# An attention loop with its score matmuls in the halves of the array's rows, four key tiles to a batch

## The chip, the cores and the metric

The kernel runs on one core of one Trainium2 chip. Its time is device time in microseconds (us). A core has five engines that run side by side and wait for one another through semaphores: TensorE (PE in the profile, with its weight loads as PEld), VectorE (DVE), ScalarE (ACT), GpSimd (POOL) and SyncE (SP), which here only issues transfers. Matmul results land in PSUM, eight banks of 128 partitions by 512 floats.

## What is computed

Two layers of a bidirectional encoder on 2048 tokens of width 1024. The part that the change touches is the attention: eight query heads of width 64, two key/value heads, all 2048 keys for every query.

```python
def _attention(q, k, v):
    ...
        scores = jnp.einsum('bqkgd,bskd->bkgqs', qb, k,
                            preferred_element_type=jnp.float32) * scale
        p = jax.nn.softmax(scores, axis=-1).astype(v.dtype)
        return jnp.einsum('bkgqs,bskd->bqkgd', p, v)
```

In each layer a combined input projection comes first, then the attention with a Fourier mixer beside it, then the output projection with a layer norm. All numbers are float32.

## The kernel before

**Stages.** `in_proj` projects the tokens (L302 to L304 and L329 to L331), writes the rotated queries to the DRAM tiles `q1`, keeps keys (`kk1`, `kk2`) and values (`V`) on the chip, and near its end runs `first_unit`, which computes the first row maxima of the attention between its own matmuls. `attention` follows, with `fourier` as a background generator: one step of it per batch, until it is through. `out_proj` comes last. Inside `attention` the queues of PE, ACT, DVE and POOL run in program order (a manual schedule); elsewhere a scheduler sets the order.

**Units and batches.** A unit is two query heads that share a key/value head, for 512 queries (`CH`): 16 units in a layer. Each unit has 16 key tiles of 128 keys, taken in six batches of 3, 3, 2, 3, 3 and 2 (`BATCHES`). For each batch PE does, one block behind the other: the scores of the batch's tiles, as many row-maxima pairs of a later unit, and the weighing by V of the tiles of the batch before.

**Scores.** Queries and keys are split into a rounded high part and a low remainder (`hi`, `lo`). A score tile of one head is two matmuls over all 128 rows of the array (L854, L855). The first has the high key twice, in rows 0 to 63 and 64 to 127, against a query tile `qq1` that holds high and low parts in its two halves. The second has the low key in one half and a row of ones in the other, against `qq2`, which holds the high query and, in one row, the negated row maximum (the guard row). ACT takes the exponential out of PSUM (L856).

**Maxima.** `row_max` computes an approximate score block with 64 rows of the array for one head and the other 64 for the other head (L789, one pair of matmuls), into two PSUM banks; DVE takes their maxima (L793). They run 6 pairs (`LEAD`) ahead of the unit whose scores come next. When a unit's 16 pairs are through, `guard_row` transposes the result on PE (L804), DVE copies it (L806), and two small transfers write it into `qq2` (L808).

**Weighing.** `weigh` multiplies the exponentials by V into 64 columns per head (L866, one PSUM bank `psC`), and adds the exponentials up for the denominators: four of a unit's tiles on DVE, twelve on POOL (L874 for the first sum, L876). In a layer's last unit all 16 are DVE's. `sums` (L885) and `finish` (L899 to L913) turn the sums into the divided result during the next unit.

**PSUM.** Seven banks (`A`) are handed out in turn to scores, maxima, sums, guard and Fourier blocks. An allocation waits until the one seven before it has been read. The eighth (`C`) holds the weighed sum of a unit.

**Names that the change touches.** `q_load` and `q_copy` (L765 to L781) load query tiles, `fourier_mix_mats` loads `fm` (L583) for four small matmuls (L591) at the end of `in_proj`.

Of the kernel before, what the change touches and what calls it, by code (L numbers as in the profile page):

```python
# [13 lines left out]
P = 128  # L14
# [24 lines left out]
class Trunk:  # L39
# [34 lines left out]
    def setup(self):  # L74
# [10 lines left out]
        self.zero = self.const("zero", [P, 4])  # L85
        nc.gpsimd.memset(self.zero, 0.0)
# [316 lines left out]
    def do_q(self, l, grp, tabs):  # L403
        def fn(ps, s0):
            qn = self.t("XA", [P, 2, 256])
            self.norm_rope(qn, ps, 4, tabs, s0 % 8)
            self.later.append(lambda: q_trans(s0 // 4, slice(s0 % 4 * P, s0 % 4 * P + 2 * P), qn))

        def q_trans(ch, sl, qn):

            nc = self.nc
            pt = self.p("C", (P, 2, 2, P))
            for r in range(2):
                for s2 in range(2):
                    nc.tensor.transpose(out=pt[:, r, s2, :], in_=qn[:, s2, r * P:(r + 1) * P], identity=self.ident)
            hi = self.t("EV", [P, 2, 2 * P], F32R)
            lo = self.t("EV", [P, 2, 2 * P], F32R)
            self.split(hi, lo, pt.rearrange("p r s n -> p r (s n)"), act=True)
            for h in range(2):
                r, o = slice(h * HD, (h + 1) * HD), slice((1 - h) * HD, (2 - h) * HD)  # L420
                nc.sync.dma_start(self.q1[ch][grp][r, :, h, sl], hi.bitcast(F32)[r])
                nc.sync.dma_start(self.q1[ch][grp][o, :, h, sl], lo.bitcast(F32)[r])
        return fn

    def do_kv(self, l, tabs):
        def fn(ps, s0):
# [16 lines left out]
            nc.vector.tensor_tensor(kl[:, :, :, HD:], k4, khf[:, :, :, 0:HD], ALU.subtract)  # L443
            kl3 = kl.rearrange("p a b d -> p (a b) d")
            nc.vector.tensor_copy(kl3[:, :, 0:1], self.ones[:, 0:4].unsqueeze(2))
            nc.vector.tensor_copy(kl3[:, :, 1:HD], self.zero.unsqueeze(2).to_broadcast([P, 4, HD - 1]))
# [313 lines left out]
    LEAD = 6  # L760
    BATCHES = ((0, 1, 2), (3, 4, 5), (6, 7), (8, 9, 10), (11, 12, 13), (14, 15))
    NBT = len(BATCHES)

    def q_load(self, u):

        src = self.q1[u["ch"]][u["pr"] // 2][:, u["pr"] % 2]
        u["qq1"] = [self.t("TAB", [P, CH], F32R) for _ in range(2)]
        for h in range(2):
            self.nc.sync.dma_start(u["qq1"][h].bitcast(F32), src[:, h, :])
        u["qq2"], u["mx"] = [], [self.small("mx", [P, 4, 4]) for _ in range(2)]  # L770
        u["nm"] = self.small("nm", [P, 2, 4], F32R, bufs=3)

    def q_copy(self, u, h):

        src = self.q1[u["ch"]][u["pr"] // 2][:, u["pr"] % 2, h, :]
        q2 = self.t("QS", [P, CH], F32R)
        for r in ([slice(0, P)] if h else [slice(0, HD), slice(HD, P)]):
            dr = r if h else slice(HD - r.start, P - r.start)
            self.nc.sync.dma_start(q2.bitcast(F32)[dr], src[r])
        u["qq2"].append(q2)  # L780

    def row_max(self, u, i):
# [4 lines left out]
        for h in range(2):  # L787
            r = slice(h * HD, (h + 1) * HD)
            nc.tensor.matmul(pss[h], u["qq1"][h][r, s * P:(s + 1) * P], self.kk1[u["kv"]][kc][r], start=True, stop=True)  # L789

        def reduce():
            for h in range(2):
                nc.vector.tensor_reduce(out=u["mx"][h][:, s, kc:kc + 1], in_=pss[h], axis=AX.X, op=ALU.max)  # L793
            if i == 15:
                for h in range(2):
                    nc.vector.tensor_reduce(out=u["nm"][:, h, :], in_=u["mx"][h], axis=AX.X, op=ALU.max, negate=True)
                self.gq.append(u)
        return reduce

    def guard_row(self, u):  # L800
# [6 lines left out]
        for h in range(2):  # L807
            nc.sync.dma_start(u["qq2"][h].bitcast(F32)[0:1, :], nt.bitcast(F32)[4 * h:4 * h + 4, :])  # L808

    def max_before(self, i):  # L810

        for ui, u in enumerate(self.units):
# [3 lines left out]
            elif o in (8, 10):  # L816
                self.q_copy(u, o // 2 - 4)

    def max_pairs(self, pairs):

        while self.gq:
            self.guard_row(self.gq.pop(0))
        todo = [self.row_max(self.units[j // 16], j % 16) for j in pairs if 0 <= j < 16 * len(self.units)]
        for reduce in todo:
            reduce()

    def first_unit(self, l):
        self.units = [dict(ch=ch, pr=pr, kv=pr // 2) for ch in range(NCH) for pr in range(NPAIR)]
        for i in range(-6, NKT + self.LEAD, 2):
            self.max_before(i)  # L830
            self.max_before(i + 1)
            self.max_pairs((i, i + 1))
            yield

# [8 lines left out]
    DVE_KT = (0, 3, 8, 11), range(NKT)  # L843

    def scores(self, u, kt):
# [5 lines left out]
        ks = slice((kt % 4) * P, (kt % 4 + 1) * P)  # L851
        for h in range(2):
            ps = self.p("A")
            nc.tensor.matmul(ps, self.kk1[kv][kt // 4][:, ks], u["qq1"][h], start=True, stop=False)  # L854
            nc.tensor.matmul(ps, self.kk2[kv][kt // 4][:, ks], u["qq2"][h], start=False, stop=True)  # L855
            nc.scalar.activation(pt[:, h, :], ps, AF.Exp, scale=HD ** -0.5)  # L856

    def weigh(self, u, kt):
# [8 lines left out]
        w = "d" if kt in self.DVE_KT[u is self.units[-1]] else "p"  # L867
        eng = nc.vector if w == "d" else nc.gpsimd
# [25 lines left out]
    def finish(self, u, k):  # L894
# [5 lines left out]
        elif k == 3:  # L900
# [4 lines left out]
            for h in range(2):  # L905
                nc.sync.dma_start(u["sm"][h * HD:(h + 1) * HD, :], d[h * CH:(h + 1) * CH].partition_broadcast(HD))
        elif k == 4:
            nc.vector.tensor_tensor(u["y"], u["y"], u["sm"], ALU.mult)
        elif k == 5:
# [5 lines left out]
    def attention(self, l):  # L915
        self.yat = {}
        n = len(self.units)
        for g in range((n + 1) * self.NBT):
            ui, b = divmod(g, self.NBT)
            u = self.units[ui] if ui < n else None  # L920
            tiles = self.BATCHES[b]
            pairs = [NKT * (ui + 1) + self.LEAD + kt for kt in tiles]
            for j in pairs:
                self.max_before(j)
            if ui and b == 2:
                self.sums(self.units[ui - 1])
            if ui == n - 1 and b == 0:
# [3 lines left out]
            if u:  # L931
                for kt in tiles:
                    self.scores(u, kt)
            self.max_pairs(pairs)
            if 0 < g <= n * self.NBT:
                v, c = divmod(g - 1, self.NBT)
                for kt in self.BATCHES[c]:
                    self.weigh(self.units[v], kt)
            if u and b == 4:
                u["ga"] = self.t("EV", [P, CH])  # L940
                self.nc.sync.dma_start(u["ga"], self.ga[u["pr"]][u["ch"]])
            if ui:
                self.finish(self.units[ui - 1], b)
# [222 lines left out]
```

## Time and profile before

| what | value |
|---|---|
| median of 3 runs | 2721.76 us (2720.47 to 2722.68) |
| profiled execution, its own time | 2718.48 us |
| its span, first to last instruction | 2716.6 us |
| mean granted TensorE clock | 0.995 |
| busy PE / DVE / ACT / POOL | 2664.5 / 1821.2 / 891.0 / 1032.7 us |

How to read the rows that stand further down: a row of the chain of waits is the start in us, the length in us, and what the end of the program hung on at that time; "x12" counts records, and a float32 matmul of the weighing has two. A row of the windows gives, for a stretch, each engine's busy time and its count of instructions. A row of the groups gives the count, the busy time in us, the mean of one in ns, and behind a bar the idle time before it with what ended it. The shape "64\*128" behind a matmul is the part of the array that it uses, rows by columns; the program's tiles "psA" are the seven PSUM banks.

### The profile page before, as it was taken

The numbers are of one execution on the slowest core, as the hardware profiler recorded it, in microseconds if no ns is written. First come the engines' busy times: TensorE is split into PE (matmuls) and PEld (weight loads), VectorE is DVE, ScalarE is ACT, GpSimd is POOL, SyncE is SP. The second block draws the span as 40 slices with busy tenths as digits, with TensorE's granted clock in tenths as the row PEclk, the third lists the DMA queues.
The fourth block names the chain that finished last, engine by engine and source line by source line (L and its number), as shares of the span: only waits on it lengthen the run. The fifth ranks groups of instructions, "written<-read, shape, count | busy, mean of one in ns | idle before, by whom it ended". The sixth has DMA issues, their size and how long they took to land.

```text
span 2716.6 us, 36918 instructions
## 1 busy us (share of the span) xinstructions
PE 2664.5 (98%) x13748; PEld 1867.2 (69%) x13748; DVE 1821.2 (67%) x3072; ACT 891.0 (33%) x1789; POOL 1032.7 (38%) x597
## 2 busy tenths in 40 slices
PE   7999999999999999999999999999999999999998
PEld 5987898765555555557898889887565555554686
DVE  6655673457788788786785347534678888778655
ACT  3321421133444444430232124211444444444200
POOL 0200020035786777703331001100558777774134
PEclk9999999999999999999999999999999999999999
DMA  9754362333221111144446123522323111111332
GB/s 302 225 138 149 108 189 72 98 101 121 80 58 44 48 48 48 36 129 156 147 132 186 55 94 98 151 79 85 111 74 105 48 48 47 45 31 51 121 132 93
DMA packets 192516, 277.34 MB, mean 102 GB/s; under 512 B 40400, under 2 KB 103248, under 8 KB 191824
## 3 DMA queue, kind: packets, MB, share of 16 engines
q1 hardware_dynamic: 192336, 274.98, 33.1%
q8 instruction: 108, 1.77, 0.3%
q14 instruction: 72, 0.59, 0.1%
HBM read 213.68 MB, written 69.48 MB: 104 GB/s over the span
## 4 chain that ended last, share of the span: by engine, by line
PE 91%; DVE 4%; DMA 2%; issue 1%; POOL 1%; ACT 1%; SPq 0%; POOLq 0%; DVEq 0%; ACTq 0%
PE psC L866 16%; PE psA L854 9%; PE psA L329 8%; PE psA L330 8%; PE psA L331 8%; PE psA L855 8%; PE psA L789 6%; PE psA L1028 4%; PE psA L1026 4%; PE psA L1027 4%; PE psA L302 3%; PE psA L304 3%; PE psA L303 3%; PE psA L885 1%; PE psA L706 1%
## 5 line engine op out<-in xcount | busy, mean ns | idle before, releaser
L793 DVE TENSOR_REDUCE mx<-psA 128x1 f32<-128x512 f32 x1024 | 632.9, 684 | 238.5 <-PE psA L789 236.3
L876 POOL TENSOR_TENSOR WH<-WH,XA 128x1024 f32<-128x1024 f32 x150 | 362.5, 2417 | 211.1 <-ACT XA L856 208.4
L854 PE MATMUL psA<-TAB,KK 128*128 128x512 f32 x1024 | 421.8, 412 | 0.0
L855 PE MATMUL psA<-QS,KK 128*128 128x512 f32 x1024 | 403.3, 394 | 0.0
L329 PE MATMUL psA<-H,WH 128*128 128x512 f32 x1008 | 397.9, 395 | 0.0
L330 PE MATMUL psA<-H,WH 128*128 128x512 f32 x1008 | 393.4, 390 | 0.0
L331 PE MATMUL psA<-H,WL 128*128 128x512 f32 x1008 | 393.0, 390 | 0.0
L876 POOL TENSOR_TENSOR WH<-WH,WL 128x1024 f32<-128x1024 f32 x150 | 361.4, 2409 | 63.2 <-ACT WL L856 53.8
L856 ACT ACTIVATE XA<-psA 128x512 f32<-128x512 f32 x512 | 281.0, 611 | 307.0 <-PE psA L855 226.3
L856 ACT ACTIVATE WL<-psA 128x512 f32<-128x512 f32 x512 | 281.6, 615 | 161.2 <-PE psA L855 161.0
L854 PEld LDWEIGHTS psA<-TAB,KK 128*128 128x128 f32 x1024 | 192.3, 188 | 155.2 <-issue 87.2
L866 PE MATMUL psC<-XA,V 128*64 128x512 f32 x1024 | 271.3, 608 | 5.8 <-DVE EV L899 5.8
L866 PE MATMUL psC<-WL,V 128*64 128x512 f32 x1024 | 267.8, 601 | 0.0
L128 DVE TENSOR_TENSOR WL<-WR,WH 128x512 fp32r<-128x512 f32 (+2 forms) x272 | 126.0, 500 | 210.0 <-ACT WH L125 204.5
L874 POOL TENSOR_TENSOR WH<-WL,XA 128x1024 f32<-128x1024 f32 x30 | 71.0, 2366 | 446.1 <-DVE mx L793 378.4
L329 PEld LDWEIGHTS psA<-H,WH 128*128 128x128 f32 x1008 | 189.6, 188 | 46.3 <-issue 7.4
L302 PE MATMUL psA<-WH,H 128*128 128x256 f32 x768 | 219.8, 287 | 0.0
L125 ACT ACTIVATE WH<-WR 128x512 fp32r<-128x512 f32 (+2 forms) x280 | 119.4, 479 | 305.3 <-PE psA L330 112.1
L855 PEld LDWEIGHTS psA<-QS,KK 128*128 128x128 f32 x1024 | 192.2, 188 | 37.7
L304 PE MATMUL psA<-WH,H 128*128 128x256 f32 x768 | 216.4, 284 | 0.6 <-DVE H L128 0.6
L303 PE MATMUL psA<-WL,H 128*128 128x256 f32 x768 | 216.8, 283 | 0.0
L331 PEld LDWEIGHTS psA<-H,WL 128*128 128x128 f32 x1008 | 189.3, 188 | 39.8
(215 smaller groups left out, 4010.5 us busy)
## 6 DMA issues: line engine op xcount, KB each, us to landing
WR<-in_w_in SPq DMA_DIRECT2D x176, 256.0 KB
WR<-in_w_ada SPq DMA_DIRECT2D x64, 256.0 KB
q<-EV SPq DMA_DIRECT2D x128, 128.0 KB
TAB<-q SPq DMA_DIRECT2D x64, 256.0 KB
H<-dft SPq DMA_DIRECT2D x64, 256.0 KB
XA<-in_x SPq DMA_DIRECT2D x24, 512.0 KB
XA<-x SPq DMA_DIRECT2D x20, 512.0 KB
dft<-in_k_dft SPq DMA_DIRECT2D x32, 256.0 KB
```

Source lines behind the costliest of these rows:

```text
L302: nc.tensor.matmul(ps[:, s2, :], hh[b][:, sl], w1, start=(b == 0), stop=False)
L303: nc.tensor.matmul(ps[:, s2, :], hh[b][:, sl], w2, start=False, stop=False)
L304: nc.tensor.matmul(ps[:, s2, :], hl[b][:, sl], w1, start=False, stop=(b == NB - 1))
L329: nc.tensor.matmul(ps, w1, hh[b], start=(b == 0), stop=False)
L330: nc.tensor.matmul(ps, w1, hl[b], start=False, stop=False)
L331: nc.tensor.matmul(ps, w2, hh[b], start=False, stop=(b == NB - 1))
L793: nc.vector.tensor_reduce(out=u["mx"][h][:, s, kc:kc + 1], in_=pss[h], axis=AX.X, op=ALU.max)
L854: nc.tensor.matmul(ps, self.kk1[kv][kt // 4][:, ks], u["qq1"][h], start=True, stop=False)
L855: nc.tensor.matmul(ps, self.kk2[kv][kt // 4][:, ks], u["qq2"][h], start=False, stop=True)
L856: nc.scalar.activation(pt[:, h, :], ps, AF.Exp, scale=HD ** -0.5)
L866: nc.tensor.matmul(u["pv"][h * HD:(h + 1) * HD, :], v, pt[:, h, :], start=(kt == 0), stop=(kt == NKT - 1))
L876: eng.tensor_tensor(acc[w], acc[w], pt, ALU.add)
```

## The change

The scores of both heads of a tile are computed side by side. Four terms, high key by high query, high key by low query, low key by high query, and a selector row by the guard row, are each a pair of matmuls, one head in rows 0 to 63 and the other in rows 64 to 127. Two PSUM banks of a tile so fill at the same time. Query tiles are kept by part (high, low) and not by head, the guard row lies in a third tile `g`, and a constant `sel` picks it. Batches are four tiles, four batches to a unit, and inside a batch score tiles (S) and maxima pairs (M) go in the order S S M S M S M M; the maxima lead by 8 pairs. POOL's additions are issued with the scores and not with the weighing, DVE adds the last tile of each batch, and `finish` is spread over the four batches and the first of the unit behind. Outside the attention the queries are written in two transfers and not four, the low key is written to both halves, and the tile `fm` has one buffer and not two.

```diff
+        self.sel = self.const("sel", [P, P], F32R)
...
-            for h in range(2):
-                r, o = slice(h * HD, (h + 1) * HD), slice((1 - h) * HD, (2 - h) * HD)
-                nc.sync.dma_start(self.q1[ch][grp][r, :, h, sl], hi.bitcast(F32)[r])
-                nc.sync.dma_start(self.q1[ch][grp][o, :, h, sl], lo.bitcast(F32)[r])
+            for j, t in enumerate((hi, lo)):
+                nc.sync.dma_start(self.q1[ch][grp][:, :, j, sl], t.bitcast(F32))
...
-            fm = self.small("fm", [P, HD], bufs=2)
+            fm = self.small("fm", [P, HD], bufs=1)
...
-    LEAD = 6
-    BATCHES = ((0, 1, 2), (3, 4, 5), (6, 7), (8, 9, 10), (11, 12, 13), (14, 15))
-    NBT = len(BATCHES)
+    LEAD = 8
+    ORDER = "SSMSMSMM"
+    BATCH = len(ORDER) // 2
+    NBT = NKT // BATCH
...
+    def guard_load(self, u):
+
+        u["g"] = self.t("QS", [P, CH], F32R)
+        self.nc.sync.dma_start(u["g"].bitcast(F32), self.q1[u["ch"]][u["pr"] // 2][:, u["pr"] % 2, 0, :])
...
+    def guard_rows(self):
+
+        for e in list(self.gq):
+            e[1] -= 1
+            if not e[1]:
+                self.guard_row(e[0])
+                self.gq.remove(e)
...
-    DVE_KT = (0, 3, 8, 11), range(NKT)
+    DVE_KT = (3, 7, 11, 15), range(NKT)
...
+        k1, k2, (q1, q2) = self.kk1[kv][kt // 4][:, ks], self.kk2[kv][kt // 4][:, ks], u["q"]
+        pss = [self.p("A") for _ in range(2)]
+        terms = (k1, q1), (k1, q2), (k2, q1), (self.sel, u["g"])
+        for i, (k, q) in enumerate(terms):
+            for h in range(2):
+                r = slice(h * HD, (h + 1) * HD)
+                nc.tensor.matmul(pss[h], k[r], q[r], start=i == 0, stop=i == len(terms) - 1)
         for h in range(2):
-            ps = self.p("A")
-            nc.tensor.matmul(ps, self.kk1[kv][kt // 4][:, ks], u["qq1"][h], start=True, stop=False)
-            nc.tensor.matmul(ps, self.kk2[kv][kt // 4][:, ks], u["qq2"][h], start=False, stop=True)
-            nc.scalar.activation(pt[:, h, :], ps, AF.Exp, scale=HD ** -0.5)
+            nc.scalar.activation(pt[:, h, :], pss[h], AF.Exp, scale=HD ** -0.5)
+        self.add(u, kt, pt, "p")
...
+            at = {"S": 0, "M": 0}
+            for c in self.ORDER:
+                if c == "M":
+                    self.max_pairs((pair + at[c],))
+                elif u:
+                    self.scores(u, first + at[c])
+                at[c] += 1
```

On PE, in the middle of a layer's attention, the end of one batch before the change: L854 and L855 are a head's two score matmuls, L789 the maxima, L866 the weighing.

```order
L854 MATMUL psA_9354<-TAB_8713,KK_778 128x512
L855 MATMUL psA_9354<-QS_9047,KK_779 128x512
L789 MATMUL psA_9358<-KK_3260,TAB_9049 128x512
L789 MATMUL psA_9359<-KK_3260,TAB_9050 128x512
L789 MATMUL psA_9362<-KK_3491,TAB_9049 128x512
L789 MATMUL psA_9363<-KK_3491,TAB_9050 128x512
L789 MATMUL psA_9366<-KK_778,TAB_9049 128x512
L789 MATMUL psA_9367<-KK_778,TAB_9050 128x512
L866 MATMUL psC_9101<-XA_9285,V_3488 64x512 x2
L866 MATMUL psC_9101<-WL_9294,V_3488 64x512 x2
L854 MATMUL psA_9394<-TAB_8712,KK_778 128x512
L855 MATMUL psA_9394<-QS_8991,KK_779 128x512
```

The same place on PE in the changed kernel: L860 is a score matmul (two heads alternate, psA_10166 and psA_10167), L786 the maxima, L873 the weighing.

```order
L786 MATMUL psA_10160<-KK_1001,TAB_9906 128x512
L860 MATMUL psA_10166<-TAB_9110,KK_3244 128x512
L860 MATMUL psA_10167<-TAB_9110,KK_3244 128x512
L860 MATMUL psA_10166<-TAB_9111,KK_3244 128x512
L860 MATMUL psA_10167<-TAB_9111,KK_3244 128x512
L860 MATMUL psA_10166<-TAB_9110,KK_3245 128x512
L860 MATMUL psA_10167<-TAB_9110,KK_3245 128x512
L860 MATMUL psA_10166<-QS_9506,sel 128x512
L860 MATMUL psA_10167<-QS_9506,sel 128x512
L786 MATMUL psA_10178<-KK_3242,TAB_9906 128x512
L786 MATMUL psA_10179<-KK_3242,TAB_9906 128x512
L786 MATMUL psA_10184<-KK_3471,TAB_9906 128x512
```

Maxima now stand between score tiles, and a tile is eight matmuls of half the rows where it was four of all rows; the weighing (four tiles of it) follows once per batch.

On SP, where the weights of the last projection groups are loaded, the rows around `fm` (L583) in the changed kernel; before, both loads of this layer stood ahead of the middle of `in_proj`, one behind the other.

```order
L272 DMA WR_5463<-in_w_in 128x2x256
L272 DMA WR_5469<-in_w_in 128x2x256
L583 DMA fm_5055<-in_f_mix 128x64
L519 DMA yc_3_139<-EV_4901 128x512
L777 DMA QS_6504<-q_0_1_88 128x512
```

The layer's second `fm` load stands here, some 200 rows later than the first, since its only buffer is read until PE has run the first two L591 matmuls.

## Rows read from the trace of the kernel before

**Rows 1.** The page's first part: busy time, share, instructions.
```profile
PE 2664.5 (98%) x13748; PEld 1867.2 (69%) x13748; DVE 1821.2 (67%) x3072; ACT 891.0 (33%) x1789; POOL 1032.7 (38%) x597
```

**Rows 2.** Windows: six units without Fourier; and the last unit of layer 0.
```profile
843.24:1066.24 223.00, 223.00 (x1065) 114.60 (x1066) 178.77 (x253) 103.28 (x204) 158.02 (x67) 1.00 0.16 44
1165.00:1190.00 25.00, 25.00 (x114) 11.39 (x112) 24.33 (x32) 11.12 (x22) 0.00 (x0) 0.94 0.38 121
```

**Rows 3.** Chain of waits, 843 to 881 us, about one unit.
```profile
843.24 1.87 PE psC L866 x8
...
848.06 0.06 PE psA L804
848.12 1.34 PE psA L789 x4
...
854.27 0.67 PE psA L789 x4
854.93 2.73 PE psC L866 x12
857.66 0.43 PE psA L854
858.09 0.24 PE psA L855
...
860.46 0.23 PE psA L855
860.69 0.90 PE psA L789 x6
...
870.05 1.00 PE psA L885 x16
```

**Rows 4.** Chain of waits, 636 to 646 us: a Fourier step (L706 to L708) before scores.
```profile
637.08 0.43 PE psA L706
...
639.80 0.23 PE psA L708
640.03 0.23 PE psA L854
```

**Rows 5.** Groups of instructions in the six units of rows 2.
```profile
L793 DVE TENSOR_REDUCE mx<-psA 128x1 f32<-128x512 f32 x193 | 119.3, 684 | 37.2 <-PE psA L789 36.5
L856 ACT ACTIVATE XA<-psA 128x512 f32<-128x512 f32 x96 | 52.7, 611 | 63.8 <-PE psA L855 39.6 <-POOL WH L876 24.2
L876 DVE TENSOR_TENSOR WH<-WH,WL 128x1024 f32<-128x1024 f32 x6 | 19.4, 3225 | 0.0
L876 DVE TENSOR_TENSOR WH<-WH,XA 128x1024 f32<-128x1024 f32 x6 | 10.7, 1782 | 0.0
```

**Rows 6.** Timeline: DVE and POOL additions, around 857 and 1150 us.
```profile
856.87 2.39 POOL L876 TENSOR_TENSOR WH<-WH,WL 128x1024 f32<-128x1024 f32 x1
857.13 3.20 DVE L876 TENSOR_TENSOR WH<-WH,WL 128x1024 f32<-128x1024 f32 x1
...
1147.73 3.26 POOL L876 TENSOR_TENSOR WH<-WH,WL 128x1024 f32<-128x1024 f32 x1
1149.23 2.31 DVE L908 TENSOR_TENSOR EV<-EV,HS 128x512 f32<-128x512 f32 x1 [0.50 <-DMA HS<-rc]
```

**Rows 7.** The maxima's weight loads, 860.6 to 861.6 us: ns min/median/max.
```profile
L789 PEld LDWEIGHTS psA<-KK,TAB x6: 182/184/186, 860.6 to 861.0; 64*128 64x128 f32 x6
```

**Rows 8.** Timeline: a score matmul, the next weight load, and its exponentials.
```profile
845.37 0.39 PE L855 MATMUL psA<-QS,KK 128*128 128x512 f32 x1
845.38 0.19 PEld L854 LDWEIGHTS psA<-TAB,KK 128*128 128x128 f32 x1
...
845.86 1.08 ACT L856 ACTIVATE WL<-psA 128x512 f32<-128x512 f32 x2 [2.75 <-PE psA L855]
```

**Rows 9.** Timeline of SP, 843 to 850 us: small transfers of a unit.
```profile
846.83 0.32 SPq L903 DMA_DIRECT2D rc<-rc  x1
848.26 1.10 SPq L906 DMA_DIRECT2D HS<-rc  x2
849.46 0.63 SPq L808 DMA_DIRECT2D QS<-HS  x1
```

**Rows 10.** Windows: a wait of PE and a stretch behind it.
```profile
1160.60:1163.40 2.80, 0.00 (x0) 0.00 (x0) 1.28 (x3) 0.80 (x2) 0.00 (x0) 1.00 0.25 91
1165.00:1167.00 2.00, 2.00 (x8) 0.30 (x4) 1.90 (x3) 0.00 (x0) 0.00 (x0) 0.50 0.34 100
```

More of the change, by code (lines that the diff above doesn't have):

```diff
@@ L442, in fn @@
             nc.vector.tensor_copy(kh[:, :, :, HD:], k4)
[L443 to L446, printed above, removed]
+            for j in range(2):
+                nc.vector.tensor_tensor(kl[:, :, :, j * HD:(j + 1) * HD], k4, khf[:, :, :, 0:HD], ALU.subtract)
             self.later.append(lambda: k_trans(ch, slice(s * P, s * P + 2 * P), kh, kl))
@@ L788, in row_max @@
             r = slice(h * HD, (h + 1) * HD)
-            nc.tensor.matmul(pss[h], u["qq1"][h][r, s * P:(s + 1) * P], self.kk1[u["kv"]][kc][r], start=True, stop=True)
-        def reduce():
+            nc.tensor.matmul(pss[h], u["q"][0][r, s * P:(s + 1) * P], self.kk1[u["kv"]][kc][r], start=True, stop=True)
+        for h in range(2):
+            nc.vector.tensor_reduce(out=u["mx"][h][:, s, kc:kc + 1], in_=pss[h], axis=AX.X, op=ALU.max)
+        if i == 15:
             for h in range(2):
[L793 to L798, printed above, removed]
+                nc.vector.tensor_reduce(out=u["nm"][:, h, :], in_=u["mx"][h], axis=AX.X, op=ALU.max, negate=True)
+            self.gq.append([u, 2])
     def guard_row(self, u):
@@ L815, in max_before @@
                 self.q_load(u)
-            elif o in (8, 10):
-                self.q_copy(u, o // 2 - 4)
+            elif o == 8:
+                self.guard_load(u)
     def max_pairs(self, pairs):
[L821 to L825, printed above, removed]
+        for j in pairs:
+            if 0 <= j < 16 * len(self.units):
+                self.row_max(self.units[j // 16], j % 16)
     def first_unit(self, l):
@@ L917, in attention @@
         n = len(self.units)
-        for g in range((n + 1) * self.NBT):
+        for g in range((n + 2) * self.NBT):
             ui, b = divmod(g, self.NBT)
             u = self.units[ui] if ui < n else None
[L921 to L925, printed above, removed]
+            first = self.BATCH * b
+            pair = NKT * (ui + 1) + self.LEAD + first
+            for j in range(self.BATCH):
+                self.max_before(pair + j)
+            if 0 < ui <= n and b == 2:
                 self.sums(self.units[ui - 1])
+            self.guard_rows()
             if ui == n - 1 and b == 0:
@@ L930, in attention @@
             self.background()
[L931 to L934, printed above, removed]
+            at = {"S": 0, "M": 0}
[5 more added lines that the diff above has]
+                at[c] += 1
             if 0 < g <= n * self.NBT:
                 v, c = divmod(g - 1, self.NBT)
-                for kt in self.BATCHES[c]:
-                    self.weigh(self.units[v], kt)
-            if u and b == 4:
+                for j in range(self.BATCH):
+                    self.weigh(self.units[v], self.BATCH * c + j)
+            if u and b == 2:
                 u["ga"] = self.t("EV", [P, CH])
                 self.nc.sync.dma_start(u["ga"], self.ga[u["pr"]][u["ch"]])
-            if ui:
-                self.finish(self.units[ui - 1], b)
+            for back in (1, 2):
+                if 0 <= ui - back < n:
+                    self.finish(self.units[ui - back], b + self.NBT * (back - 1))
     def wout_consts(self, l):
```

38 lines of the change are left out of this document (19 added, 19 removed).

## Prediction

> **What bounds the kernel now.** I read the page's busy shares first: PE is busy 98% of the span, DVE 67% [rows 1]. Then the windows, because shares mix stages: the change works inside the attention, and six of its units without Fourier work take 223.00 us, 37.17 each, with PE busy for all of it, DVE for 178.77 / 6 = 29.8 and POOL for 26.3 us a unit [rows 2]. So PE sets the pace there, and the question is what of PE's 37.17 us is not work. The chain of waits tells it [rows 3]. A score matmul costs 0.23 to 0.24 us behind another, but 0.43 when it is the first behind the weighing. Two pairs of maxima take 0.67 us and three take 0.90: 0.23 a pair, two heads side by side, plus 0.20 for coming in. Four records per tile of the weighing give 1.87 us for two tiles and 2.73 for three: 0.86 a tile, plus 0.15. The 0.20 is no price of a first matmul as such: scores that follow a Fourier step, which uses the whole array as they do, cost 0.23 at once, while the Fourier step behind the weighing paid 0.43 [rows 4]. So **each change of the array's shape costs PE 0.15 to 0.20 us**, and a batch has three of them: 18 a unit. In the last unit of a layer, however, DVE has all the additions and is busy 24.33 of 25.00 us [rows 2]; there PE's saving buys nothing.
>
> Put together, the rows rebuild the unit. A batch of three: 0.43 + 11 x 0.235 + 0.90 + 2.73 = 6.65; of two: 0.43 + 7 x 0.235 + 0.67 + 1.87 = 4.62; four and two of them are 35.8; sums 1.00, guard 0.06, and 0.44 that one batch waits before its maxima (1.34 where others take 0.90): 37.3, against 37.17 measured.
>
> **The changed unit.** Scores and maxima now have one shape, 64 rows by 128, so a batch has two changes of shape and a unit has eight. I carry one batch along from its start. A pair of half-array matmuls is taken at 0.235 us, the maxima's price. A tile is four pairs, 0.94, as much as its four whole-array matmuls before, so **the work itself saves nothing**. With 0.20 for coming in, tiles one and two end at 1.14 and 2.08, the first maxima at 2.31, tile three at 3.25, the second maxima at 3.48. ACT sees a result about 0.26 after its matmul's slot (start 845.37, slot 0.23, ACT at 845.86 [rows 8]) and takes 52.7 / 96 = 0.55 for an exponential [rows 5]: 1.40 to 2.50 for tile one, to 3.60 for tile two. Tile four wants to begin at 3.48, but its first bank is the eleventh handed out, so it needs the fourth, tile two's second head, read at 3.60: it begins at about 3.65, **a new wait of 0.17 a batch**. It ends at 4.59, the last two maxima at 5.06, and the weighing at 5.06 + 0.15 + 4 x 0.86 = 8.65. DVE takes 119.3 / 193 = 0.62 for a maximum [rows 5]: from 2.57 to 7.55 for the eight, then its addition.
>
> That addition needs care. DVE's addition beside POOL's took 3.20: POOL's ended at 859.26 and DVE's 1.07 later [rows 6]; those in another place took 10.7 / 6 = 1.78 [rows 5]. So DVE's addition waits for the POOL one under way and then takes 1.07. POOL's three additions of a batch, 2.39 each, run from 2.5 to about 9.7, so DVE's ends at 10.8, 2.1 into the next batch and before that batch's first maxima at 2.57. With the short pieces of `finish` DVE is free by 3.0, and the bank that waits for the first maximum is wanted at 3.65. DVE so hides, with half a microsecond to spare; if that cover goes, PE waits at tile four.
>
> Unit: 4 x 8.65 + 1.00 for sums + 0.26 for the guard transpose, which now has a shape of its own between weighing and scores = 35.9. Against the 37.3 rebuilt from the same rows that is **1.4 us less a unit**. It holds for 14.5 of a layer's 16 units (in the second half of the fifteenth no maxima are left, and the last is DVE's), so 29 units: -40.6 us.
>
> **What the change adds.** Fourier matmuls use the whole array; they used to lead into scores of the same shape, now 16 steps a layer (eight small and eight large, of the generator) pay one more change: 32 x 0.20 = +6.4. The second `fm` load now waits for PE's first two L591 matmuls, and PE, next in order, waits for it. A small transfer of the profile takes 1.43 us from its issue to that of the one that needs its data (846.83 to 848.26 [rows 9]); the bounds are 1.4 and 2.8 with a busy queue. After a PE wait of 2.80 us the granted clock stood at 0.50, the lower level, 1.2 GHz, from 1165 to 1167 [rows 10], at least 1 us more. I take 2.5 a layer, +5.0, between +2.8 and +8. One more step of maxima in `in_proj` is +0.4 a layer, +0.8.
>
> Hidden: POOL's additions are issued a batch earlier, DVE loses small copies in `in_proj` and queries are written in half as many transfers; none of these stands in the chain. The guard row has less room. Its transpose begins a unit's last batch, DVE copies it at about 2.7, and SP has the reciprocals' transfers ahead of it: 846.83 to 849.46 is 2.63 [rows 9]. From 2.4 that makes 5.0, 1.3 to issue two, about 1.4 to land: 7.7, while the first selector matmul comes at 8.9 + 0.9. Two us are left; before it was about six.
>
> **Sum.** -40.6 + 6.4 + 5.0 + 0.8 = -28.4. The profiled execution's own time, 2718.48, becomes 2690.1; the median of the runs lies 3.28 above that execution, so I forecast **2693**. Bounds of this case: no wait at tile four (29 x 4 x 0.17 = 20), half-array pairs at 0.23 (29 x 64 x 0.005 = 9), and the small load at 1.4, together 2662; pairs at 0.243 (29 x 80 x 0.008 = 19) and the large load at 2.8 plus clock, 2715.
>
> **Rivals.** *Nothing gained.* Maxima show two or three pairs in a row, never twenty. If each of 80 pairs a unit costs 0.247, 29 x 80 x 0.012 = 28 us are gone: 2721. Against it: three pairs show no growth over two.
>
> *DVE turns into the bound; slower.* DVE has some 31 us of 35.9 to fill, and its two-input additions wait for POOL's. If DVE's addition is passed over once more, its batch's maxima begin 2.4 us late, tile four waits until about 5.5 and loses 1.9. One such batch a unit turns -1.4 into +0.5: 2722 + 29 x 0.5 + 12 = 2748; in all three batches with an addition about 2850. It decides as soon as DVE is free later than 3.1 us into a batch. For it: POOL has the same 26.3 us to do in 35.9 instead of 37.2. Against it: where POOL's additions stood back to back, each engine let the other through after one (POOL 3.26, then DVE 2.31 [rows 6]). The Trainium skill, "SBUF — State Buffer", "SBUF: two separate sides", calls the shared port pair an exclusive lock for whichever instruction starts first; the 3.20 agrees, and the page says nothing on who is next.
>
> *Weight loads no longer hide; much slower.* A weight load of 64 rows takes 0.184 us [rows 7], and a score pair needs one per head. Had they to wait for the matmuls in their own rows, 64 pairs a unit would each pay 0.184 more: 32 x 64 x 0.184 = 377, less the 28: about 3070. Against it: the load at 845.38 ran under the matmul that began at 845.37 in the same rows [rows 8], and maxima pairs follow at 0.23. The Trainium skill, "TensorE: Matmul & The Clock Gate", "Part 3: Packing small matmuls — row/col tiling", states just this rule, that a weight load overlaps matmuls in flight only if its row group differs; the trace speaks against it.
>
> *More than forecast*, below 2662: all of these bounds at once, and additions that meet POOL's less often than now.
>
> **How the numbers follow.** The forecast has 0.62, nothing gained (2716 to 2727) 0.14, the DVE bound 0.13, weight loads 0.03, more than forecast 0.08. The range takes in the forecast's bounds and the no-gain case, and some of the greater gain: 2655 to 2728. About 0.2%, 5.4 us, is what a measurement of this kernel can tell from no change. Faster by more than that (below 2716.3) is the forecast and the greater gain, 0.70; within it 0.14, slower 0.16.
>
> **What would show it.** Right: units of 35.5 to 36.3 us in the windows; in the chain, a first score of 0.43 behind the weighing and no 0.20 at the maxima between score tiles; waits of tile four for ACT near 0.2; a PE gap of some 2 us at L591. Wrong: score pairs far from 0.235 in a long row; PE waiting for DVE's maxima in most batches; PE waiting for the guard row at a unit's start; or an end of the attention that loses what the units gained.

## The result and the profile after

The changed kernel takes 2685.62 us, median of 4 runs (2684.45 to 2688.34); the kernel before took 2722.22 beside it. The ratio is 0.987, with a 95% interval of 0.985 to 0.989: 36.6 us faster where 28.8 were forecast, and inside the range. The profiled execution of after is its slowest, 2688.34 (span 2686.6), that of before lies 3.7 under its median, so the two traces show 30 us of the 36.6.

The page's first part stands against [rows 1]: about 2,000 more matmuls, and 34 us less of busy PE.

```profile
PE 2630.2 (98%) x15796; PEld 1885.8 (70%) x15796; DVE 1783.2 (66%) x3057; ACT 909.7 (34%) x1789; POOL 1079.0 (40%) x599
```

A window of one unit without Fourier work, against the first of [rows 2] (us; then busy time of PE, PEld, DVE, ACT, POOL, with counts; clock; DMA share; GB/s):

```profile
950.19:985.57 35.38, 35.38 (x243) 19.49 (x245) 28.32 (x43) 17.86 (x34) 28.00 (x12) 1.00 0.13 39
```

The next one takes 35.39, the usual unit: 1.78 less than the 37.17 of before; PE is still never idle. The chain of waits through one batch (start, us, what; L860 the scores, L786 the maxima, L873 the weighing), against [rows 3]:

```profile
864.86 2.04 PE psA L860 x16
866.90 0.23 PE psA L786 x2
867.14 0.93 PE psA L860 x8
868.06 0.23 PE psA L786 x2
868.29 1.09 PE psA L860 x8
869.39 0.47 PE psA L786 x4
869.86 3.58 PE psC L873 x16
```

From 864.86 to the end of the weighing at 873.44 is 8.58, where the forecast had 8.65. Tiles one and two take 2.04, seven pairs at 0.23 and the first at 0.43; the maxima between score tiles take 0.23 with nothing for coming in; tile four takes 1.09 where tile three takes 0.93, which is 0.16 where a wait of 0.17 was forecast.

Cut at the first score and at the first `out_proj` matmul, the two spans differ as follows: start to first attention +7.0, first attention -22.1 (622.4 to 600.3), between +5.2, second attention -22.7, last `out_proj` +2.5. Together -30.1.

### The profile page after: what moved, and what is told of

Read it like the earlier page. It is cut to its first block, busy times and chain, and to the rows that moved or that the text cites. A ratio compares the mean times of both kernels' runs of the same rounds, so it can differ in the third digit from the quotient of the medians.

```text
span 2686.6 us, 40969 instructions
## 1 busy us (share of the span) xinstructions
PE 2630.2 (98%) x15796; PEld 1885.8 (70%) x15796; DVE 1783.2 (66%) x3057; ACT 909.7 (34%) x1789; POOL 1079.0 (40%) x599
## 4 chain that ended last, share of the span: by engine, by line
PE 88%; DVE 6%; DMA 2%; POOL 1%; issue 1%; ACT 1%; SPq 0%; POOLq 0%; DVEq 0%; ACTq 0%
PE psA L860 18%; PE psC L873 16%; PE psA L333 9%; PE psA L334 8%; PE psA L335 8%; PE psA L786 4%; PE psA L306 3%; PE psA L1045 3%; PE psA L308 3%; PE psA L1043 3%; PE psA L307 3%; PE psA L1044 3%; PE psA L897 1%; DVE mx L789 1%; POOL XA L1016 1%
## 5 line engine op out<-in xcount | busy, mean ns | idle before, releaser
L789 DVE TENSOR_REDUCE mx<-psA 128x1 f32<-128x512 f32 x1024 | 631.4, 681 | 228.7 <-PE psA L786 227.0
L888 POOL TENSOR_TENSOR WH<-WH,XA 128x1024 f32<-128x1024 f32 x210 | 553.1, 2634 | 194.0 <-ACT XA L862 184.4
L860 PE MATMUL psA<-TAB,KK 64*128 64x512 f32 x3072 | 471.5, 407 | 1.5 <-ACT XA L862 0.7
L860 PEld LDWEIGHTS psA<-TAB,KK 64*128 64x128 f32 x3072 | 275.2, 184 | 138.5 <-issue 40.6
L873 PE MATMUL psC<-XA,V 128*64 128x512 f32 x1024 | 269.6, 605 | 0.0
L873 PE MATMUL psC<-WL,V 128*64 128x512 f32 x1024 | 263.1, 592 | 0.0
L886 POOL TENSOR_TENSOR WH<-XA,WL 128x1024 f32<-128x1024 f32 x30 | 71.6, 2387 | 440.5 <-ACT WL L862 440.5
L333 PEld LDWEIGHTS psA<-H,WH 128*128 128x128 f32 x1008 | 190.3, 189 | 47.1 <-issue 8.1
L334 PEld LDWEIGHTS psA<-H,WH 128*128 128x128 f32 x1008 | 190.0, 188 | 37.8
L888 POOL TENSOR_TENSOR WH<-WH,WL 128x1024 f32<-128x1024 f32 x90 | 213.0, 2366 | 7.1
L860 PE MATMUL psA<-QS,sel 64*128 64x512 f32 x1024 | 206.2, 388 | 0.0
```

Source lines behind the costliest of these rows:

```text
L333: nc.tensor.matmul(ps, w1, hh[b], start=(b == 0), stop=False)
L334: nc.tensor.matmul(ps, w1, hl[b], start=False, stop=False)
L860: nc.tensor.matmul(pss[h], k[r], q[r], start=i == 0, stop=i == len(terms) - 1)
L873: nc.tensor.matmul(u["pv"][h * HD:(h + 1) * HD, :], v, pt[:, h, :], start=(kt == 0), stop=(kt == NKT - 1))
L888: eng.tensor_tensor(acc[w], acc[w], pt, ALU.add)
```

## Experiments

Each time is a median, with the ratio to the kernel before on the same chip (2718.1 to 2719.7 in these runs). A "unit" below is the time from one start of ACT's copy of a unit's sums (L900) to the next, in the timeline. The ten units of a layer between the Fourier work and the last two are compared. The changes of shape are those between scores, maxima and weighing; the sums and the guard transpose are left out.

| kernel | shape changes a unit | usual unit, us | other ones | time, us | ratio |
|---|---|---|---|---|---|
| before | 18 | 37.1 to 37.2 | 37.3 to 37.4 | 2722.2 | |
| changed | 8 | 35.39 | 35.5 to 36.2 | 2685.6 | 0.985 to 0.989 |
| order in turn, full-array scores | 28 | 38.71 | none | 2760.6 | 1.014 to 1.017 |
| full-array scores, blocks of four | 12 | 38.8 to 39.1 | 40.5 to 40.8 | 2775.5 | 1.019 to 1.022 |
| half-array scores, blocks of four | 8 | 39.40 | 39.7 | 2794.8 | 1.027 to 1.030 |
| batches of two | 16 | 37.96 | 38.4; 36.8 to 37.0 | 2748.1 | 1.009 to 1.012 |
| one tile in turn | 8 | 36.14 to 36.2 | 36.3 to 37.1 | 2699.9 | 0.992 to 0.995 |

**What a change of shape costs.** The kernel before, with its full-array scores, in batches of four and in the changed kernel's order (DVE's tiles and the steps of `finish` stand where the changed kernel has them; of the edit only the order is shown):

```
...
+            at = {"S": 0, "M": 0}
+            for c in "SSMSMSMM":
+                if c == "M":
+                    self.max_pairs((pairs[at[c]],))
+                elif u:
+                    self.scores(u, tiles[at[c]])
+                at[c] += 1
...
```

> The kernel before with its full-array scores, in batches of four tiles and in the changed kernel's order (two score tiles, a maxima tile, a score tile, a maxima tile, a score tile, two maxima tiles). Work and order on PE are the changed kernel's; only the scores keep the other array shape, so that each place where scores and maxima meet is a change of shape: seven a batch, 28 a unit, where the changed kernel has 8. My theory (each change 0.15 to 0.20 us): +20 x 0.18 = 3.6 us a unit over the changed kernel's 35.39, about 39.0, or 29 x 3.6 + 0 = +104 us, near 2785. In the chain the first score behind a maxima pair takes 0.43 in place of 0.24, and a maxima pair between scores 0.4 in place of 0.23. Rival: the order in turn is what gains and shape changes between half and whole array are hidden, units near 35.5 to 36.5, 2685 to 2715.

It took 2760.6. Its chain, one batch:

```profile
917.43 0.43 PE psA L854
917.87 0.23 PE psA L855
...
919.51 0.43 PE psA L789 x2
919.95 0.43 PE psA L854
...
922.61 0.67 PE psA L789 x2
```

Every first score or maxima pair behind another shape takes 0.42 to 0.44 where the same takes 0.23 behind its own: 0.20, six times a batch. The seventh change, into the weighing, costs 0.15 in both kernels (3.58 for four tiles at 0.86). The batch is 9.43 against 8.58, the unit 38.71 against 35.39: 3.32 for 20 changes is 0.17 each, net. In full it is 0.20: tile four's wait has gone, since PE comes later and ACT has time, and 20 x 0.20 less 4 x 0.16 is 3.36. So the theory holds. The time of the whole is 75 us up and not 104. Units with Fourier work grew by 2.6 only (45.9 against 43.4): here the four Fourier steps of such a unit lead into scores of their own shape, which saves 4 x 0.20. And this kernel has no wait for `fm`.

The weight loads (PEld) in the timeline of this run show where the 0.20 goes:

```profile
918.88 0.40 PE L854 MATMUL psA<-TAB,KK 128*128 128x512 f32 x1
918.88 0.19 PEld L855 LDWEIGHTS psA<-QS,KK 128*128 128x128 f32 x1
919.12 0.40 PE L855 MATMUL psA<-QS,KK 128*128 128x512 f32 x1
919.44 0.18 PEld L789 LDWEIGHTS psA<-KK,TAB 64*128 64x128 f32 x2 [0.37 <-issue]
919.44 0.50 PE L789 MATMUL psA<-KK,TAB 64*128 64x512 f32 x2
```

Between equal shapes the next weight load begins with the matmul before it (L855's at 918.88) and is hidden under it. At the change to the maxima it begins 0.32 behind the start of the matmul before (919.44 against 919.12), together with its own matmul. So it is in this trace from 830 to 1110 us at each of the some 190 changes between scores, maxima and weighing: 0.32 to 0.52 behind, where within one shape it is 0.01 at most. What keeps the load back is not shown.

**Batches of two.** The guard row, the sums, the Fourier steps and `finish` keep their places in a unit (of the edit only the order is shown):

```
-    ORDER = "SSMSMSMM"
+    ORDER = "SSMM"
...
```

> The changed kernel with eight batches of two key tiles a unit in place of four of four: two score tiles, two maxima tiles, then the weighing of two tiles. Work is the same; the array changes its shape 16 times a unit in place of 8. If a change of shape costs 0.15 to 0.20 us as the rows of before showed, a unit is 8 x 0.18 = 1.4 us longer, less what the waits of tile four gave (4 x 0.17 = 0.7 us): +0.7 to +1.4, or +20 to +41 us, 2706 to 2727. Rival: the gain of the change comes from scores and maxima taken in turn, and shape changes are hidden or cheap: within 5 us of 2686. Another: shorter batches leave ACT and DVE less time between a score and the weighing that needs its exponentials, so PE waits for DVE or ACT: over 2740.

It took 2748.1. The chain's undisturbed batch:

```profile
806.28 2.04 PE psA L860 x16
808.33 0.46 PE psA L786 x4
808.79 1.87 PE psC L873 x8
```

And the largest row of PE's waits that the changed kernel doesn't have (us, times, longest), with the chain through two batches that DVE holds up:

```profile
PE psC L873 <- DVE EV L911: 14.7, 27, 3.3
```

```profile
837.21 2.65 DVE H L132
839.86 2.40 DVE mx L789 x4
...
842.30 0.50 PE psA L786 x2
```

Eight batches of 4.37, 1.00 for sums and 0.15 for the guard make 36.1, 0.7 over the changed kernel, as the price of eight changes less four waits of tile four has it. The other 1.85 of its 37.96 are DVE's. Some 0.5 of them a unit is the row above (14.7 over 27); the rest are maxima and scores that wait for banks which DVE still has to read, behind its addition and the steps of `finish`: from 823 to 842 us the chain runs through DVE. Both the theory and the last rival were needed; neither alone gives 2748.

**Fewer batches alone, with scores as before.** Batches of four tiles, scores as one block and the maxima behind them, on the whole array (the later steps of a unit stand as in the changed kernel; only the batches are shown) and on halves of it:

```
-    LEAD = 6
-    BATCHES = ((0, 1, 2), (3, 4, 5), (6, 7), (8, 9, 10), (11, 12, 13), (14, 15))
+    LEAD = 8
+    BATCHES = ((0, 1, 2, 3), (4, 5, 6, 7), (8, 9, 10, 11), (12, 13, 14, 15))
...
```

> The kernel before with its full-array scores, cut into four batches of four key tiles a unit (lead of eight maxima tiles, the later steps of a unit and DVE's tiles spread as in the changed kernel). Changes of the array's shape fall from 18 to 12 a unit; scores still come as one block and the maxima as another. If only the number of shape changes and batches counts, a unit saves 6 x 0.185 = 1.1 us, 29 x 1.1 = 32 us: about 2690. If the order in turn is a part of the gain, four score tiles in a row run ahead of ACT (0.55 us an exponential against 0.47 for a score), the maxima behind them wait for banks as they did in the order of blocks with half-array scores, where a batch took 9.4 us instead of 8.57: 0.4 to 0.8 a batch, 29 x 4 x 0.6 = 70 us the other way, 2735 to 2790.

```
-    ORDER = "SSMSMSMM"
+    ORDER = "SSSSMMMM"
```

> The changed kernel with four score tiles first and then the four maxima tiles in each batch. Changes of the array's shape stay at eight a unit, so the theory that the gain is only the fewer changes has this at the changed kernel's time, about 2686. The theory of the walk: ACT needs 0.55 us for an exponential where PE makes a score in 0.47, and no maxima stand between to let ACT catch up, so the score tiles three and four and then the maxima wait for banks, about 1.2 us a batch for 29 x 4 batches less what is hidden, +80 to +140 us: 2765 to 2825.

They took 2775.5 and 2794.8: in both the second mechanism that was expected. The chain of the second, and one weight load of its maxima in the timeline:

```profile
909.66 3.89 PE psA L860 x32
913.55 1.83 PE psA L786 x8
915.38 3.58 PE psC L873 x16
```

```profile
913.91 0.18 PEld L786 LDWEIGHTS psA<-KK,TAB 64*128 64x128 f32 x1 [0.31 <-ACT XA L862]
```

Four pairs of maxima take 1.83 where 4 x 0.23 would do. The chain gives no engine for the gap, but the loads do: three of them wait 0.30 to 0.31 each, and what ends each wait is an exponential of ACT, as the prediction's walk through the banks had it. The batch is 9.3 for 8.58. Four of them, sums and guard make 38.4 of the 39.40; most of the rest is one batch a unit whose maxima wait for DVE as well. In the first kernel ACT's exponentials stand in the chain, and a batch's maxima take 1.71 where 0.20 + 4 x 0.23 would do. So the order in turn is no gain over before's small batches, by these sums, but what makes batches of four possible: with blocks, fewer changes lose more than they save.

**One tile in turn.**

```
-    ORDER = "SSMSMSMM"
+    ORDER = "SMSMSMSM"
```

> The changed kernel with the order score, maxima, score, maxima, ... (one tile of each in turn) in place of two score tiles, maxima, a score tile, maxima, a score tile, two maxima. The walk through the banks: tile four no longer waits 0.17 for its first bank, which is 29 x 4 x 0.17 = 20 us less, about 2666. Rival: DVE gets its first maximum to read a tile earlier but must also be free a tile earlier; where its addition or a finish step is still under way (0.7 us in one or two batches of a unit) PE waits for it, which takes back all or more: 2685 to 2705. A third: the banks are handed out in another order and the maxima now wait for the exponentials of the tile before, 0.5 a tile or more: over 2720.

It took 2699.9: the second mechanism that was expected. PE's waits (us, times, longest) show DVE's maxima:

```profile
PE psA L860 <- DVE mx L789: 12.9, 20, 1.2
```

And the wait that should go only moved, to tile three (1.04), as the chain shows:

```profile
913.45 0.93 PE psA L860 x8
...
914.60 1.04 PE psA L860 x8
```

**Are two heads really side by side?** First the four matmuls of one head, then those of the other:

```
-        for i, (k, q) in enumerate(terms):
-            for h in range(2):
+        for h in range(2):
+            for i, (k, q) in enumerate(terms):
```

> The changed kernel with the four score matmuls of the first head issued before the four of the second, in place of the two heads in turn. If two matmuls run side by side only where neighbours in the order use different halves of the rows, a tile takes eight slots of 0.23 (1.84 us) in place of four pairs (0.93), and the weight loads, no longer in turn either, may add to that: 32 units x 16 tiles x 0.9 = 460 us, about 3150. Rival: PE's queues run far enough ahead for the halves to overlap whatever the order within a tile: about 2686.

It took 2681.2 in its one run, and its chain has the same 0.93 for a tile, with 2.15 for the first two where the turn has 2.04. The second fence is the timeline of its first tile:

```profile
932.73 2.15 PE psA L860 x16
...
935.11 0.93 PE psA L860 x8
```

```profile
932.66 0.97 PE L860 MATMUL psA<-TAB,KK 64*128 64x512 f32 x6
933.46 0.40 PE L860 MATMUL psA<-QS,sel 64*128 64x512 f32 x2
```

My theory fell. The program has a head's selector matmul (`sel`) fourth and the other head's eighth; in the trace both come last, 0.01 us apart. So the second half of the rows runs ahead of the program's order. The run left open whether halves overlap or a half-array matmul is simply half as long, so both heads were put in the same rows (both are then computed from the first head's queries and keys; the kernel leaves out the second head's):

```
-                r = slice(h * HD, (h + 1) * HD)
+                r = slice(0, HD)
```

> The changed kernel with both heads' score matmuls in the first half of the rows (both heads are computed from the first head's queries and keys; count and shapes of all instructions stay). It settles what the run with the heads one after the other left open: whether a tile of eight half-array matmuls takes 0.93 us because two run side by side, or because a half-array matmul by itself takes half the time. Side by side: nothing can pair here, a tile takes 8 x 0.23 = 1.84, 32 x 16 x 0.91 = 466 us more, about 3150; if the weight load of 0.184 can't hide under a matmul of its own rows either, up to 8 x 0.184 more a tile, about 3900. Half the time each: 0.93 a tile, about 2686.

It took 3127.1:

```profile
1096.35 1.39 PE psA L860 x6
```

Its weight loads (ns min/median/max):

```profile
L860 PEld LDWEIGHTS psA<-TAB,KK x48: 183/185/188, 1079.8 to 1099.2; 64*128 64x128 f32 x48
```

A score matmul now costs 0.23 by itself (1.39 / 6), a tile 1.86. So the halves do run side by side, and the order of the heads within a tile doesn't decide it. The price of 0.23 also has the weight load of 0.185 hidden under matmuls of its own rows, as long as the shape stays the same.

**The waits at `fm`.** Both halves of `f_mix` loaded ahead:

```
+        fms = self.t("HS", [P, 2, HD])
         for b in range(2):
-            fm = self.small("fm", [P, HD], bufs=1)
-            nc.sync.dma_start(fm, self.f_mix[l, 2 * b:2 * b + 2].rearrange("g c d -> (g c) d"))
+            nc.sync.dma_start(fms[:, b, :], self.f_mix[l, 2 * b:2 * b + 2].rearrange("g c d -> (g c) d"))
+        for b in range(2):
+            fm = fms[:, b, :]
```

> The changed kernel, but both halves of f_mix are loaded ahead into one tile, so that the second small load no longer waits for PE's first two L591 matmuls. My theory: in the trace of the changed kernel PE stood some 2.4 us a layer at L591 for the transfer, and in one layer its next matmuls ran at a granted clock of 0.50 (0.43 us where others take 0.23); the whole term is 5 to 8 us, so this kernel takes 5 to 8 us less than the changed one, 2678 to 2681. Rival: PE's wait there is made up for later (the units that follow wait less for their tiles), and the time stays within 2 us of the changed kernel's, about 2685.

It took 2679.0 (ratio 0.984 to 0.987). Against the changed kernel's trace the first sums come 5.3 us earlier, and from the last sums of the first layer to the first of the second it is 3.5 less. PE's wait at this line is gone. The ratios' intervals overlap, so the size rests on the traces.

**Where eleven of the twenty units lose 0.15 to 0.85.** The next three runs stand on that kernel and concern DVE. First `L920` on POOL:

```
-            nc.vector.tensor_tensor(u["y"], u["y"], u["sm"], ALU.mult)
+            nc.gpsimd.tensor_tensor(u["y"], u["y"], u["sm"], ALU.mult)
```

> The changed kernel with both halves of f_mix loaded ahead, and the multiplication of L920 issued on POOL in place of DVE. My theory (DVE's L920 waiting for POOL is what makes ten units 0.3 to 0.8 us longer): they go, 2672 to 2676. Rival: POOL, which is late in just those units, gets 1.3 us more of work a unit, ends its additions later, and DVE's addition or the sums wait for it: 2679 to 2690.

It took 2672.4, ratio 0.981 to 0.984, below the changed kernel's whole interval and just below that of the kernel that it stands on (0.984 to 0.987); only the last of the three runs is as fast. The delays shrank but did not go: over both layers the ten units exceed 35.38 by 5.4 us in the changed kernel, by 3.1 here, and of these 1.9 are in the first of the ten, which grew to 36.34. The last unit of a layer, DVE's, is 0.4 to 1.9 shorter than in the kernel that it stands on. Then, in its place, DVE's tiles moved:

```
-    DVE_KT = (3, 7, 11, 15), range(NKT)
+    DVE_KT = (1, 3, 7, 15), range(NKT)
```

> The changed kernel with both halves of f_mix loaded ahead (the run that took 2679.0), and DVE's four tiles of a unit moved from 3, 7, 11, 15 to 1, 3, 7, 15, so that the batch with the multiplication of L920 has no addition of DVE. My theory: the units of 35.7 to 36.2 us, where most take 35.39, are those in which POOL has other work, is late with its additions, and L920 waits for one of them behind DVE's own addition, so that the next batch's maxima are late; ten such units are worth about 5 us: 2672 to 2676, all units near 35.4. Rival: the additions meet POOL's at another place and the delay only moves: 2677 to 2685. A third: POOL has four tiles in a row in one batch, 9.6 us for a batch of 8.57, frees the exponentials' tiles late, and ACT and then PE wait: over 2685.

It took 2690.2, worse as the third way had it, but ACT was not what waited. POOL and SP's queue in the timeline, beginning with a unit's last batch (843.46), and then the chain:

```profile
847.83 1.29 POOL L739 TENSOR_TENSOR H<-H,H 128x512 f32<-128x512 f32 x1
```

```profile
849.14 0.32 SPq L740 DMA_DIRECT2D yf<-H  x1
849.56 0.38 SPq L917 DMA_DIRECT2D rc<-rc  x1
...
852.61 1.30 SPq L805 DMA_DIRECT2D QS<-HS  x2
```

```profile
852.61 2.46 DMA QS<-HS
```

With four of its tiles in a row POOL reaches the Fourier tail's multiplication 4.4 into the batch; SP's store of it waits for that, and behind the store the reciprocals' transfers (the reciprocal itself had ended at 843.26) and the guard row's. The first selector matmul waits, in four places of this run, 7.8 us together, longest 2.2. In the changed kernel the guard row's transfers of the same unit are issued 6.7 us behind its cast (847.08 to 853.77), here 9.1. Last, with `L920` on POOL as above, the casts for `w_out` on ACT:

```
-        self.split(hi, lo, raw, act=n == 1)
+        self.split(hi, lo, raw, act=True)
```

> The changed kernel with both halves of f_mix loaded ahead and L920 on POOL (the run that took 2672.4), and the cast that makes the upper part of w_out's first half issued on ACT in place of DVE. My theory: at the end of each attention PE waits 3.3 us for DVE's last additions and runs its next matmuls at a granted clock of 0.50; DVE loses eight casts of 0.35 to 0.44 us there, so the wait shrinks to about 1 us: 2 to 3 us a layer, 2664 to 2669. Rival: what ends there last is the load of w_out's blocks or the reciprocals' transfers, and the time stays, 2671 to 2674. A third: the casts on ACT stand between exponentials and make PE wait for banks: over 2674.

PE's wait for DVE at the end of the first attention fell from 3.3 to 2.1, and the time stayed, 2672.4, as the rival had it. What the shorter wait is worth is too small to be told.

**POOL's additions a batch later**, as before the change:

```
-        self.add(u, kt, pt, "p")
...
         self.add(u, kt, pt, "d")
+        self.add(u, kt, pt, "p")
```

> The changed kernel with POOL's additions issued again where the weighing is, a batch later than in the changed kernel. My theory: that part of the change is hidden (POOL has 26.3 us to do in 35.4), so the time stays, 2683 to 2690. Rival: the earlier place matters, since the sums of a unit wait for POOL's last addition at the third batch of the next unit and the tiles that hold exponentials come free later: PE or ACT waits, over 2692.

It took 2685.1: that part of the change is hidden, as forecast.

## Why the prediction held, and where its terms were off

**The main term** was right in kind and too small. Ten changes fewer a unit, eight at 0.20 and two at 0.15, are 1.9, and a unit lost 1.78. The other differences nearly cancel: four waits of tile four (+0.64) and the guard transpose (+0.09) against the 0.44 that before waited at its maxima and 64 scores at 0.231 instead of some 0.234 (-0.2). The experiments with 16 and 28 changes ask the same price. The forecast told it by rows, as a price; that it is a weight load which no longer hides was not in it. The forecast had 1.4. Its changed unit of 35.9 was 0.5 too long: 0.3 is the pair (0.23, not 0.235, or 0.08 a batch), 0.11 the guard transpose (0.15, not 0.26). Its rebuilt unit of before was 0.13 too long, which gives a little back. Over 29 units the 0.38 are 11 us.

**Tile four's wait** was there, 0.16 for 0.17. That taking it out would give 20 us, a part of my lower bound, did not come: in the order of one tile in turn 0.11 of it moved to tile three, and DVE took back more.

**DVE hides** in most units, but the walk had its order wrong. I had its addition wait for POOL's third; it gets in behind the second, and the multiplication of `finish` behind it waits instead. The timeline of DVE and POOL in the changed kernel, in a unit in which POOL has a step of the Fourier tail besides:

```profile
817.96 1.90 DVE L888 TENSOR_TENSOR WH<-WH,WL 128x1024 f32<-128x1024 f32 x1
819.79 2.90 DVE L920 TENSOR_TENSOR EV<-EV,HS 128x512 f32<-128x512 f32 x1
...
816.43 2.36 POOL L888 TENSOR_TENSOR WH<-WH,WL 128x1024 f32<-128x1024 f32 x1
818.86 3.27 POOL L888 TENSOR_TENSOR WH<-WH,XA 128x1024 f32<-128x1024 f32 x1
```

And the chain behind it:

```profile
823.34 1.19 PE psA L860 x7
...
825.04 3.58 PE psC L873 x16
```

DVE's addition ends 1.07 behind POOL's second, the same as in [rows 6], and `L920` ends half a microsecond behind POOL's third. The batch would begin at 810.83 + 8.57 = 819.40; DVE is free 3.3 us into it, past the 3.1 that I had as the point, and the weighing begins 5.64 in instead of 4.99. This is the slower rival in small. I had priced a batch so struck at 1.9 and put one in each unit, 55 us; it was 0.15 to 0.85 in eleven units of the twenty that can be compared, 5.4 us. That it stayed so small is not what the walk gave.

**Fourier** was right where it can be read, in the chain:

```profile
655.72 0.43 PE psA L706
...
658.70 2.04 PE psA L860 x16
```

The step pays for coming in, and so does the first pair of scores behind it, which paid nothing before [rows 4]. Taking 29 x 1.78 = 51.6, and 5.4 and 6.4 against it, 39.8 of the 44.8 that the two attentions lost are told. The rest lies at a layer's end. From the first score of one unit to that of the next, the last two units of a layer are 2.1 and 3.4 us shorter in the two layers, though two more tiles of weighing (1.71) are left for them than before; the forecast had 0.9 for them, and nothing for the last. That is 7 us more than forecast, and the first fourteen units give 2 back. One wait of before is gone there, PE's for `finish` (L866 for DVE's L899, 5.8 us in both layers), while that for DVE's last additions grew from 4.8 to 8.6. What sets the balance stays open.

**`fm`** was right in kind; its clock was the larger half in one layer. The chain in the first layer:

```profile
495.73 2.24 DMA fm<-in_f_mix
...
498.10 1.08 PE psA L591 x4
...
499.71 0.43 PE psA L334
```

And two windows, one behind the wait in each layer (columns as above):

```profile
498.00:500.00 2.00, 1.90 (x7) 1.74 (x8) 1.72 (x6) 0.00 (x0) 0.00 (x0) 0.50 0.84 152
...
1816.00:1820.00 4.00, 3.85 (x19) 3.31 (x20) 1.76 (x6) 0.00 (x0) 0.00 (x0) 1.00 0.78 233
```

PE stood 2.4 us a layer. In the first layer the granted clock then stood at 0.50, the level of 1.2 GHz, until 504.3: eleven matmuls took 0.43 for 0.23, and with the L591 and the first behind them, slower too, that stretch took 2.9 more than the same one of the second layer, where the clock stayed at 1.00. Together 7.7 where I took 5.0, within its bounds of 2.8 and 8.

**The guard row** came in time, but not with the two us that I had left. DVE copied it at once (847.08, where I had 2.7 into the batch), yet SP began to issue its transfers 6.7 into the batch, where I had 5.0: a store of the Fourier tail (850.28) and the reciprocals' transfers stand ahead of them.

```profile
853.77 1.30 SPq L803 DMA_DIRECT2D QS<-HS  x2
```

In the run with DVE's tiles moved, 2.4 later cost a wait of up to 2.2, so some 0.2 us was left here. It is so in four units, those with this store at that place; in the others the transfers are issued four us and more ahead of the first selector matmul.

**What I had not listed:** the end of the attention. DVE's last additions hold PE as before, but now its first `out_proj` matmuls run at the lower clock (granted 0.50 from 1179 to 1183), where those of before took 0.23 from the second on:

```profile
1178.57 0.73 PE psA L1043
1179.30 0.43 PE psA L1044
```

Ten at 0.43, one between and a first of 0.73 for 0.43 are 2.4 us; the second layer loses 2.2 in the same way. That is most of the +2.5 at the end, and with 2.4 at `fm` most of the +5.2 between. Of the +7.0 at the start `fm` tells 5.3; the rest is open.

**The rivals.** Nothing gained fell, since pairs are 0.23 over twenty in a row. Weight loads that don't hide fell too, within one shape: with everything in the same rows a matmul still takes 0.23 with a load of 0.185 for each. The rule weighed there (the Trainium skill, "TensorE: Matmul & The Clock Gate", "Part 3: Packing small matmuls — row/col tiling") says that a load overlaps matmuls in flight only in other rows; the measurement says otherwise.

The median gained 8 us more than forecast and the traces 1.6: errors of both signs (-11 for the unit, -5 at the ends of attention, +5.4 for DVE, +9 outside it) nearly cancel in the profiled executions. That is luck in part; the main term was right, and too small. The rest is the place of those executions among their runs.

## What to carry to other kernels

Count, per pass of the inner loop, how often the array changes its shape, and price each at the difference between a first instruction and the next like it in the chain. Before making batches longer to save them, walk the banks: where a producer runs ahead of its reader, the saving is lost unless the second kind of work is set between. And where an engine hides, look which short step stands behind its additions, and which transfers stand behind that on SP.

## What the runs showed of the chip

- A change of array shape costs 0.20 us in the chain into scores or maxima and 0.15 into the weighing, 0.17 net in the unit; a full-array matmul and a pair of half-array ones both cost 0.23 to 0.24.
- At a change of shape between scores, maxima and weighing the weight load does not begin with the matmul before: it comes 0.32 to 0.52 us behind that one's start, where within one shape it is 0.01 at most (order in turn with full-array scores, 830 to 1110 us).
- Halves of the array overlap even where the program names four matmuls of one half before the four of the other: 0.93 a tile either way. The trace then has the second half ahead of the program's order; what lets it run ahead was not found.
- A weight load of 0.185 hides under matmuls of its own rows and shape at 0.23 each.
- Behind the same wait of 2.4 us the granted clock fell to 0.50 until 6 us after it in one layer and stayed at 1.00 in the other.
